# FFN up projection as seven products of halves, with the activations through DRAM and the down projection in a phase of its own

## The chip, the cores and the metric

The kernel runs on one core of a Trainium2 chip. The metric is the time of one execution in microseconds. A core has TensorE (PE in the profile; PEld are its weight loads), VectorE (DVE), ScalarE (ACT), GpSimd (POOL) and SyncE (SP), whose queue issues all DMAs here. Each engine works through its own queue in order, and semaphores make it wait for others. Products accumulate in PSUM, which has 8 banks of 512 float32 columns; all else lies in SBUF.

## The reference

It is one step of a small decoder of two layers over T = 1056 tokens (1024 of a prompt, and 8 samples of 4). Each layer has a mixer, a convolutional FFN and a gated embedding. The change is in the FFN, D = 1024 wide inside, 2 x 2816 = 5632 after the up projection:

```python
def conv_ffn(xn, prefix, w_up, conv_w, conv_b, w_down):
    L = xn.shape[1]
    u = xn @ w_up
    ext = jnp.concatenate([prefix.astype(u.dtype), u], axis=1)
    c = conv_b + ext[:, 0:L] * conv_w[0]
    for k in range(1, CONV_W):
        c = c + ext[:, k:k + L] * conv_w[k]
    gate, val = jnp.split(c, 2, axis=-1)
    return (jax.nn.gelu(gate) * val) @ w_down, ext[:, -CONV_BUF:]

xn = rmsnorm(h, W['norm_ffn'][i])
f, cstate = conv_ffn(xn, cpre, W['w_up'][i], W['conv_w'][i], W['conv_b'][i], W['w_down'][i])
h = h + f
```

## The kernel before

Everything is kept with features on the 128 partitions and tokens along the free axis. The state `h` is 8 tiles of 128 x 1056 in SBUF; its gained copy is kept as a high part `xh` and a low part `xl` (rounded to fp32r and the rest), and weights are split into `wh` and `wl` in the same way by `split` (L140 on ScalarE, L141 on VectorE). A product of two float32 matrices is then three matmuls: wh with xh, wh with xl, wl with xh. The norm's factor `R` per token is applied when a product is taken out of PSUM.

`product` (L157) makes one output tile of 128 features over three chunks of C = 352 tokens in three PSUM banks: for each of the k input tiles and each of the three terms, three matmuls of 352 columns. `product1` (L163 to L165) makes one chunk after the other, where a stage begins or ends.

`ffn` runs over 11 groups g. A group has two units; `unit(i)` makes gate tile i and value tile 22 + i:

- `up` loads 1024 x 128 of `w_up` (512 KB), splits it, makes 72 matmuls into one of two three-bank PSUM tiles `mm`, and VectorE multiplies them by R into `ext` (L563, L565, L566). GpSimd copies the conv's state columns (L568 to L570).
- `conv` starts on ScalarE (L574) and adds two taps on VectorE (L576). The gate's result goes through gelu (L582), VectorE multiplies gate by value (L585), and the activation is split into `ah` and `al` (L588, L589, L592), which stay in SBUF.

Between the two units of a group, `down(g - 1)` multiplies the activations of the group before by two rows of 128 of `w_down`: 8 output tiles of 18 matmuls, each added to h by VectorE (L624). The last `down` runs chunk by chunk with the next norm (`finish`, `factor`). `embed` and `cached_keys` turn small inputs beside the groups.

Layer 0's FFN follows the pooling mixer, whose last step (`chunk`, L366 to L381) adds to h and makes xh and xl and the squares for the norm. Layer 1's follows the attention's output projection, in which the last of 8 tiles is done chunk by chunk and `finish` is called for all 8 tiles behind it. GpSimd adds the squares (L221, L381). Within the stages a scheduler orders each engine's queue by program order and its own forecast of when inputs are ready; the list `late` holds back the first weight blocks behind the pooling.

## Time and profile before

| | us |
|---|---|
| median of 3 runs (2300.02 to 2303.77) | 2303.06 |
| the profiled execution | 2297.09 |
| its span, first to last instruction | 2295.3 |
| TensorE busy / weight loads | 2257.1 / 2209.3 |
| VectorE busy | 1368.8 |
| ScalarE busy | 820.5 |
| GpSimd busy | 458.2 |
| mean granted TensorE clock | 0.993 |

The layers' FFNs lie at about 95 to 850 us and 1385 to 2160 us. Busy shares are averages over stages with different limits, so the engines are read by stretches. A matmul's own duration includes the time that it shares with its neighbours; what one costs is the distance between the starts of two.

### The profile page before, as it was taken

The numbers are of one execution on the slowest core, as the hardware profiler recorded it, in microseconds if no ns is written. First come the engines' busy times: TensorE is split into PE (matmuls) and PEld (weight loads), VectorE is DVE, ScalarE is ACT, GpSimd is POOL, SyncE is SP. The second block draws the span as 40 slices with busy tenths as digits, with TensorE's granted clock in tenths as the row PEclk, the third lists the DMA queues.
The fourth block names the chain that finished last, engine by engine and source line by source line (L and its number), as shares of the span: only waits on it lengthen the run. The fifth ranks groups of instructions, "written<-read, shape, count | busy, mean of one in ns | idle before, by whom it ended". The sixth has DMA issues, their size and how long they took to land.

```text
span 2295.3 us, 34410 instructions
## 1 busy us (share of the span) xinstructions
PE 2257.1 (98%) x14037; PEld 2209.3 (96%) x14037; DVE 1368.8 (60%) x2122; ACT 820.5 (36%) x1489; POOL 458.2 (20%) x584
## 2 busy tenths in 40 slices
...
DMA packets 199265, 133.09 MB, mean 58 GB/s; under 512 B 36356, under 2 KB 183509, under 8 KB 198940
## 3 DMA queue, kind: packets, MB, share of 16 engines
...
## 4 chain that ended last, share of the span: by engine, by line
PE 84%; DVE 8%; ACT 3%; DMA 1%; POOL 1%; issue 1%; SPq 0%; ACTq 0%; POOLq 0%; DVEq 0%
PE mm L157 65%; DVE xl L212 2%; PE ub L163 2%; PE ub L164 2%; PE ub L165 2%; PE qkp L163 1%; PE qkp L165 1%; PE qkp L164 1%; PE dps L320 1%; DVE wl L141 1%; DVE h L634 1%; ACT e L964 1%; PE aux L163 1%; PE aux L165 1%; PE aux L164 1%
## 5 line engine op out<-in xcount | busy, mean ns | idle before, releaser
L157 PE MATMUL mm<-xh,wh 128*128 128x352 f32 x2208 | 477.4, 324 | 0.4 <-DVE ext L566 0.4
L157 PE MATMUL mm<-xh,wl 128*128 128x352 f32 x2208 | 476.3, 323 | 0.2 <-DVE wl L141 0.2
L157 PE MATMUL mm<-xl,wh 128*128 128x352 f32 x2208 | 475.5, 323 | 0.0
L140 ACT ACTIVATE wh<-wr 128x1024 fp32r<-128x1024 f32 x166 | 175.7, 1059 | 739.8 <-PE mm L157 623.4
L157 PEld LDWEIGHTS mm<-xh,wl 128*128 128x128 f32 x2208 | 378.9, 188 | 0.7 <-DVE wl L141 0.5
L157 PEld LDWEIGHTS mm<-xh,wh 128*128 128x128 f32 x2208 | 375.9, 189 | 0.7 <-issue 0.6
L157 PEld LDWEIGHTS mm<-xl,wh 128*128 128x128 f32 x2208 | 374.8, 188 | 0.6 <-issue 0.6
L563 DVE TENSOR_TENSOR ext<-mm,R 128x704 f32<-128x704 f32 x88 | 78.5, 892 | 474.9 <-PE mm L157 466.8
L569 POOL COPY sto<-ext 128x2 f32<-128x2 f32 x88 | 103.7, 1178 | 970.9 <-DVE ext L565 970.9
L624 DVE TENSOR_TENSOR h<-mm,h 128x1056 f32<-128x1056 f32 x160 | 200.9, 1256 | 115.7 <-PE mm L157 115.1
L141 DVE TENSOR_TENSOR wl<-wr,wh 128x1024 fp32r<-128x1024 f32 x164 | 204.2, 1246 | 9.6 <-ACT wh L140 8.9
L157 PE MATMUL mm<-ah,wh 128*128 128x352 f32 x960 | 208.1, 325 | 0.0
L157 PE MATMUL mm<-al,wh 128*128 128x352 f32 x960 | 207.3, 324 | 0.0
L157 PE MATMUL mm<-ah,wl 128*128 128x352 f32 x960 | 205.8, 323 | 0.0
L157 PEld LDWEIGHTS mm<-ah,wl 128*128 128x128 f32 x960 | 163.6, 188 | 0.0
L157 PEld LDWEIGHTS mm<-al,wh 128*128 128x128 f32 x960 | 163.3, 188 | 0.0
L157 PEld LDWEIGHTS mm<-ah,wh 128*128 128x128 f32 x960 | 162.3, 188 | 0.3
L163 PE MATMUL ub<-xh,wh 128*128 128x352 f32 x432 | 141.9, 328 | 0.1
L165 PE MATMUL ub<-xh,wl 128*128 128x352 f32 x432 | 140.1, 324 | 0.0
L164 PE MATMUL ub<-xl,wh 128*128 128x352 f32 x432 | 139.0, 322 | 0.0
L221 POOL TENSOR_TENSOR acc<-acc,sq 128x352 f32<-128x352 f32 x84 | 94.5, 1127 | 195.8 <-ACT sq L220 193.5
L576 DVE SCALAR_TENSOR_TENSOR cg<-ext,cw,cg 128x1072 f32<-128x1072 f32 x88 | 117.4, 1334 | 16.1 <-ACT cg L574 14.7
...
## 6 DMA issues: line engine op xcount, KB each, us to landing
...
```

The source lines that it names most:

```text
L140: A.activation(out=wh, in_=flat, func=AF.Copy)
L141: (low or V).tensor_tensor(out=wl, in0=flat, in1=wh.bitcast(F32), op=ALU.subtract)
L157: PE.matmul(ps[:, c, :C], w[k], b[k][:, c * C:(c + 1) * C], start=st, stop=sp)
L163: PE.matmul(ps, wh[k], bh[k][:, cs], start=k == 0, stop=False)
L164: PE.matmul(ps, wh[k], bl[k][:, cs], start=False, stop=False)
L165: PE.matmul(ps, wl[k], bh[k][:, cs], start=False, stop=k == nk - 1)
L212: V.scalar_tensor_tensor(out=xl[:, m, cs], in0=hm, scalar=gains[:, gain, m:m + 1], in1=xh[:, m, cs].bitcast(F32), op0=ALU.mult, op1=ALU.su ...
L221: G.tensor_tensor(out=st["acc"][:, cs], in0=st["acc"][:, cs], in1=sq, op=ALU.add)
L563: V.tensor_tensor(out=e[:, 2:2 + 2 * C].rearrange("p (c n) -> p c n", n=C), in0=ps[:, 0:2, :C], in1=R[:, :2 * C].rearrange("p (c n) -> p c ...
L569: G.tensor_copy(out=sto[:, j, 0:2], in_=e[:, NP:NP + 2])
L576: V.scalar_tensor_tensor(out=c, in0=e[:, k:k + CO], scalar=cw[:, k, j:j + 1], in1=c, op0=ALU.mult, op1=ALU.add)
L624: V.tensor_tensor(out=three(f.h[:, m, :]), in0=ps[:, :, :C], in1=three(f.h[:, m, :]), op=ALU.add)
```

## The change

The up product of a unit, gate tile over value tile, is a 2 x 2 block product: the 256 output features are two blocks, the 1024 input features two halves of four k tiles, and the tokens two halves of H = 528 (N1, N2). Seven products of halves with sums take the place of eight. GpSimd makes the four sums of weight halves, VectorE the four sums of token halves (`token_sums`, once per layer, into xh, xl, the buffers of h and `t4h`, `t4l`), and all sums are split into high and low parts. A product (`prod`) is 24 matmuls of HC = 264 columns into a PSUM tile of two banks; there are three such tiles, x, y and z, and two products accumulate in each before it is used again. ScalarE copies two products, VectorE adds and multiplies by R, and GpSimd multiplies the second token half by R (`second`).

The activation of each unit is stored in DRAM (`ad`). All 22 units of a layer run first; then the buffers of the up phase are given up, h is read back from `hd` (its SBUF held token sums meanwhile; the pooling and the output projection now store it there), and the 11 down groups run in a phase of their own, each reading its two activations back and splitting them (`act_in`). h is kept as four tiles of two features each (`hm_`) for this. In the output projection, the squares for the norm are taken tile by tile. What `up` and the old `unit` held is left out here.

```diff
+    def kept(m, c):
+        return slice(c * C, (c + 1) * C if m >= DT // 2 else min((c + 1) * C, H))
+    def high_part(f, m, cs, gain):
+        return A.activation(out=xh[:, m, cs], in_=hm_(f, m)[:, cs], func=AF.Identity, scale=gains[:, gain, m:m + 1])
+    def low_part(f, m, cs, gain):
+        V.scalar_tensor_tensor(out=xl[:, m, cs], in0=hm_(f, m)[:, cs], scalar=gains[:, gain, m:m + 1],
+                               in1=xh[:, m, cs].bitcast(F32), op0=ALU.mult, op1=ALU.subtract)
...
                 for m in ms:
-                    act = A.activation(out=xh[:, m, cs], in_=f.h[:, m, cs], func=AF.Identity, scale=gains[:, g_ffn[0], m:m + 1])
+                    dma(hd[m, :, cs], hm_(f, m)[:, cs])
+                for m in ms:
+                    if c < 2 or m >= DT // 2:
+                        act = high_part(f, m, kept(m, c), g_ffn[0])
...
+        sch, scl = wide("sch"), wide("scl")
+        t4h, t4l = [fp.tile([P, 4, H], F32R, name=n) for n in ("t4h", "t4l")]
+        vh, vl = wide("vh", 512), wide("vl", 512)
+        for n in ("p1", "p5", "u2", "vv"):
+            wide(n, H, F32)
+        exts = [fp.tile([P, EXT], F32, name=f"ext{i}") for i in range(2)]
+        wide("cg", CO, F32)
+        wide("S", 2048, F32)
+        sin = fp.tile([P, UT, 16], F32, name="sin", tag="sin", bufs=1)
+        wide("cv", CO, F32)
         sto = fp.tile([P, UT, 32], F32, name="sto", tag="sto", bufs=1)
         raw = fp.tile([P, UT, 32], F32, name="stg", tag="stg", bufs=1)
...
+        x_ps, y_ps, z_ps = [us.tile([P, 2, 512], F32, name=n)[:, :, :HC] for n in "xyz"]
...
+        def after_late():
+            es = ExitStack()
+            for ins in late:
+                es.enter_context(tc.issue_after(ins.ins))
+            return es
+        def parts_of(src, h_, l_):
+            A.activation(out=h_, in_=src, func=AF.Copy)
+            V.tensor_tensor(out=l_, in0=src, in1=h_.bitcast(F32), op=ALU.subtract)
+            return h_, l_
+        def rows(w):
+            return [x.rearrange("p (k m) -> p k m", m=P) for x in w]
+        def load(i):
+            g, v = [wp.tile([P, 1024], F32, name="wr") for _ in range(2)]
+            for x, j in ((g, i), (v, FT + i)):
+                dma(x.rearrange("p (k m) -> p k m", k=DT), a["w_up"][l].rearrange("(k p) m -> p k m", p=P)[:, :, j * P:(j + 1) * P])
+            S = wide("S", 2048, F32)
+            with after_late():
+                G.tensor_tensor(out=S[:, 0:512], in0=v[:, A1], in1=v[:, A2], op=ALU.add)
+                G.tensor_tensor(out=S[:, 512:1024], in0=S[:, 0:512], in1=g[:, A1], op=ALU.subtract)
+                G.tensor_tensor(out=S[:, 1024:1536], in0=g[:, A1], in1=v[:, A1], op=ALU.subtract)
+                G.tensor_tensor(out=S[:, 1536:2048], in0=g[:, A2], in1=S[:, 512:1024], op=ALU.subtract)
+            return g, v, S
+        def gate_parts(w):
+            with after_late():
+                return rows(parts_of(w[0], wp.tile([P, 1024], F32R, name="wh"), wp.tile([P, 1024], F32R, name="wl")))
+        def s34_parts(w):
+            with after_late():
+                return rows(parts_of(w[2][:, 1024:2048], wp.tile([P, 1024], F32R, name="wh"), wp.tile([P, 1024], F32R, name="wl")))
+        def s12_parts(w):
+            with after_late():
+                return rows(parts_of(w[2][:, 0:1024], wide("sch"), wide("scl")))
+        def val_parts(w):
+            with after_late():
+                return rows(parts_of(w[1][:, A2], wide("vh", 512), wide("vl", 512)))
+        def token_sums():
+            for k in range(4):
+                K = k + 4
+                gK = gains[:, gain, K:K + 1]
+                b = wide2("act")
+                A.activation(out=b, in_=hm_(f, k), func=AF.Identity, scale=gains[:, gain, k:k + 1])
+                ta, tb = exts if k % 2 else (wide("cg", CO, F32), wide("cv", CO, F32))
+                t1, t2, t3, t4 = ta[:, 2:2 + H], ta[:, 2 + H:2 + T], tb[:, 2:2 + H], tb[:, 2 + H:2 + T]
+                V.tensor_tensor(out=t1, in0=b[:, N2], in1=b[:, N1], op=ALU.subtract)
+                V.scalar_tensor_tensor(out=t2, in0=hm_(f, K)[:, N2], scalar=gK, in1=t1, op0=ALU.mult, op1=ALU.subtract)
+                V.scalar_tensor_tensor(out=t3, in0=hm_(f, K)[:, N2], scalar=gK, in1=b[:, N2], op0=ALU.mult, op1=ALU.subtract)
+                V.scalar_tensor_tensor(out=t4, in0=hm_(f, K)[:, N1], scalar=gK, in1=t2, op0=ALU.mult, op1=ALU.subtract)
+                tk = f.hp.tile([P, 2, T], F32R, name="tk", tag="h", bufs=4)
+                tks.append(tk)
+                for t, h_, l_, eng in ((t1, xh[:, k, N2], xl[:, k, N2], G), (t2, tk[:, 0, N1], tk[:, 0, N2], V),
+                                       (t3, tk[:, 1, N1], tk[:, 1, N2], G), (t4, t4h[:, k, :], t4l[:, k, :], V)):
+                    A.activation(out=h_, in_=t, func=AF.Copy)
+                    eng.tensor_tensor(out=l_, in0=t, in1=h_.bitcast(F32), op=ALU.subtract)
+        def wide2(name):
+            return fp.tile([P, T], F32, name=name, tag=name, bufs=2)
+        B11 = ([xh[:, k, N1] for k in range(4)], [xl[:, k, N1] for k in range(4)])
+        B21 = ([xh[:, k, N1] for k in range(4, 8)], [xl[:, k, N1] for k in range(4, 8)])
+        B22 = ([xh[:, k, N2] for k in range(4, 8)], [xl[:, k, N2] for k in range(4, 8)])
+        T1 = ([xh[:, k, N2] for k in range(4)], [xl[:, k, N2] for k in range(4)])
+        T2, T3 = [([], []), ([], [])]
+        T4 = ([t4h[:, k, :] for k in range(4)], [t4l[:, k, :] for k in range(4)])
+        def prod(ps, w, k0, b, first, by_chunk=False):
+            terms = [(k, x, y) for k in range(4) for x, y in ((w[0], b[0]), (w[0], b[1]), (w[1], b[0]))]
+            order = [(n, c) for c in range(2) for n in range(12)] if by_chunk else [(n, c) for n in range(12) for c in range(2)]
+            for n, c in order:
+                k, x, y = terms[n]
+                PE.matmul(ps[:, c, :], x[:, k0 + k, :], y[k][:, c * HC:(c + 1) * HC], start=first and n == 0, stop=n == 11,
+                          skip_group_check=True)
+        def unit(i, wa, wc, wb, wv):
+            R = f.R
+            R1, R2, RS = two(R[:, N1]), R[:, H:NP], R[:, NP:].rearrange("p (s t) -> p s t", t=LS)
+            ew, ev = exts
+            nxt_w = []
+            def tmp(n):
+                return wide(n, H, F32)
+            def second(j, e, src):
+                es = e[:, 2 + NP:].rearrange("p (s u) -> p s u", u=6)
+                G.tensor_tensor(out=e[:, 2 + H:2 + NP], in0=src[:, :NP - H], in1=R2, op=ALU.mult)
+                G.tensor_tensor(out=es[:, :, 2:6], in0=src[:, NP - H:].rearrange("p (s t) -> p s t", t=LS), in1=RS, op=ALU.mult)
+                G.tensor_copy(out=es[:, :, 0:2], in_=sin[:, j, :].rearrange("p (s r) -> p s r", r=2))
+                G.tensor_copy(out=sto[:, j, 0:2], in_=e[:, NP:NP + 2])
+                G.tensor_copy(out=sto[:, j, 2:18].rearrange("p (s r) -> p s r", r=2), in_=es[:, :, 4:6])
+            p1, p5, u2, vv = [tmp(n) for n in ("p1", "p5", "u2", "vv")]
+            more = i + 1 < FT
+            prod(x_ps, wa, 0, B11, True, i == 0)
+            A.activation(out=two(p1), in_=x_ps, func=AF.Copy)
+            if more:
+                raw_w = load(i + 1)
+            if i:
+                prod(y_ps, wc, 4, T2, True)
+                V.tensor_tensor(out=two(u2), in0=y_ps, in1=two(p1), op=ALU.add)
+                prod(z_ps, wc, 0, T1, True)
+                A.activation(out=two(p5), in_=z_ps, func=AF.Copy)
+                if more:
+                    wc_ = s12_parts(raw_w)
+                prod(x_ps, wa, 4, B21, False)
+                V.tensor_tensor(out=two(ew[:, 2:2 + H]), in0=x_ps, in1=R1, op=ALU.mult)
+                if more:
+                    wa_ = gate_parts(raw_w)
+                prod(y_ps, wb, 0, T3, False)
+            else:
+                prod(z_ps, wb, 4, B22, True)
+                A.activation(out=two(p5), in_=z_ps, func=AF.Copy)
+                prod(x_ps, wa, 4, B21, False)
+                V.tensor_tensor(out=two(ew[:, 2:2 + H]), in0=x_ps, in1=R1, op=ALU.mult)
+                wa_ = gate_parts(raw_w)
+                prod(z_ps, wc, 0, T1, False)
+                V.tensor_tensor(out=two(p5), in0=z_ps, in1=two(p5), op=ALU.subtract)
+                prod(y_ps, wc, 4, T2, True)
+                V.tensor_tensor(out=two(u2), in0=y_ps, in1=two(p1), op=ALU.add)
+                wc_ = s12_parts(raw_w)
+                prod(y_ps, wb, 0, T3, False)
+            V.tensor_tensor(out=two(vv), in0=y_ps, in1=two(p1), op=ALU.add)
+            V.tensor_tensor(out=vv, in0=vv, in1=p5, op=ALU.add)
+            second(FT + i, ev, vv)
+            if i:
+                prod(z_ps, wb, 4, B22, False)
+            V.tensor_tensor(out=two(u2), in0=z_ps, in1=two(u2), op=ALU.add)
+            second(i, ew, u2)
+            if more:
+                wb_ = s34_parts(raw_w)
+            prod(y_ps, wv, 0, T4, False)
+            V.tensor_tensor(out=two(p1), in0=y_ps, in1=two(p1), op=ALU.add)
+            V.tensor_tensor(out=ev[:, 2:2 + H], in0=p1, in1=R[:, N1], op=ALU.mult)
+            if more:
+                wv_ = val_parts(raw_w)
+            cg = conv(i, ew, "cg")
+            A.activation(out=cg, in_=cg, func=AF.Gelu_apprx_tanh)
+            cv = conv(FT + i, ev, "cv")
+            act = wide2("act")
+            V.tensor_tensor(out=act[:, :NP], in0=cg[:, :NP], in1=cv[:, :NP], op=ALU.mult)
+            V.tensor_tensor(out=act[:, NP:].rearrange("p (s t) -> p s t", t=LS), in0=bass_rows(cg), in1=bass_rows(cv), op=ALU.mult)
+            dma(ad[i], act)
+            return (wa_, wc_, wb_, wv_) if more else None
+        def conv(j, e, name):
+            c = wide(name, CO, F32)
+            A.activation(out=c, in_=e[:, 0:CO], func=AF.Identity, scale=cw[:, 0, j:j + 1], bias=cw[:, 3, j:j + 1])
+            for k in (1, 2):
+                V.scalar_tensor_tensor(out=c, in0=e[:, k:k + CO], scalar=cw[:, k, j:j + 1], in1=c, op0=ALU.mult, op1=ALU.add)
+            return c
+        def bass_rows(c):
+            v = c[:, NP + 2:CO]
+            return bass.AP(v.tensor, v.offset, [v.ap[0], [6, NS], [1, LS]])
+        w = load(0)
+        w = (gate_parts(w), s12_parts(w), s34_parts(w), val_parts(w))
+        tks = []
+        token_sums()
+        for x, q in ((T2, 0), (T3, 1)):
+            x[0].extend(t[:, q, N1] for t in tks)
+            x[1].extend(t[:, q, N2] for t in tks)
...
+        late.clear()
+        for i in range(FT):
+            w = unit(i, *w)
+        V.transpose(raw.rearrange("p t c -> p (t c)"), sto.rearrange("p t c -> p (t c)"))
+        dp = o["conv_p"][l, 0].rearrange("r (t q c) -> q r t c", q=4, c=32)
+        ds = o["conv_s"][l].rearrange("s r (t q c) -> q (s r) t c", q=4, c=32)
+        pairs(f)
+        for m in range(DT):
+            dma(hm_(f, m), hd[m])
+        for q in range(4):
+            dma(dp[q], raw[32 * q:32 * q + 2])
+            dma(ds[q], raw[32 * q + 2:32 * q + 18])
+        fes.close()
+        ues.close()
...
+        def act_in(i):
+            r = dn.tile([P, T], F32, name="ar", tag="ar", bufs=2)
+            dma(r, ad[i])
+            ah, al = [tp.tile([P, T], F32R, name=n, tag="aa", bufs=8) for n in ("ah", "al")]
+            acts[i] = parts_of(r, ah, al)
...
         ng = FT // 2
         for g in range(ng):
+            act_in(2 * g)
+            act_in(2 * g + 1)
             if g in (2, 3, 4):
-                embed(l, f, fp, range(3 * g - 6, 3 * g - 3))
+                embed(l, f, dn, range(3 * g - 6, 3 * g - 3))
             if l == 0 and g in (5, 6):
                 for j in range(2):
-                    cached_keys(f, fp, g - 5, j)
-            unit(2 * g)
-            late.clear()
-            if g and g < ng - 1:
+                    cached_keys(f, dn, g - 5, j)
+            if g:
+                if g == ng - 1:
+                    des.close()
                 down(g - 1, False)
-            unit(2 * g + 1)
-        down(ng - 2, False)
-        V.transpose(raw.rearrange("p t c -> p (t c)"), sto.rearrange("p t c -> p (t c)"))
-        dp = o["conv_p"][l, 0].rearrange("r (t q c) -> q r t c", q=4, c=32)
-        ds = o["conv_s"][l].rearrange("s r (t q c) -> q (s r) t c", q=4, c=32)
-        for q in range(4):
-            dma(dp[q], raw[32 * q:32 * q + 2])
-            dma(ds[q], raw[32 * q + 2:32 * q + 18])
-        fes.close()
         down(ng - 1, True)
+        return tp
 
 
     def embed(l, f, fp, ts):
@@ -699,7 +896,7 @@
 
     def ple_start(l, f, fp):
 
-        parts = [[fp.tile([P, T], F32R, name=n, tag=n, bufs=4) for _ in range(2)] for n in ("ah", "al")]
+        parts = [[fp.tile([P, T], F32R, name=n, tag="aa", bufs=8) for _ in range(2)] for n in ("ah", "al")]
...
                     product(ps, *ops)
-                    V.tensor_tensor(out=three(f.h[:, m, :]), in0=ps[:, :, :C], in1=three(f.h[:, m, :]), op=ALU.add)
+                    V.tensor_tensor(out=three(hm_(f, m)), in0=ps[:, :, :C], in1=three(hm_(f, m)), op=ALU.add)
+                    dma(hd[m], hm_(f, m))
+                    for c in range(3):
+                        finish(f, fp, m, c, None, st)
                     continue
...
-                        finish(f, fp, i, c, g_ffn[1], st)
+                        if c < 2 or i >= DT // 2:
+                            high_part(f, i, kept(i, c), g_ffn[1])
+                            low_part(f, i, kept(i, c), g_ffn[1])
                     factor(f, fp, st, c)
```

## Rows read from the trace of the kernel before

**Rows 1.** The page: busy by engine; the chain that ended last, by engine.
```profile
PE 2257.1 (98%) x14037; PEld 2209.3 (96%) x14037; DVE 1368.8 (60%) x2122; ACT 820.5 (36%) x1489; POOL 458.2 (20%) x584
...
PE 84%; DVE 8%; ACT 3%; DMA 1%; POOL 1%; issue 1%; SPq 0%; ACTq 0%; POOLq 0%; DVEq 0%
```
**Rows 2.** Windows, FFN of layer 0: length; busy PE, PEld, DVE, ACT, POOL; PEclk, DMA, GB/s.
```profile
300.00:400.00 100.00, 100.00 (x621) 100.00 (x620) 58.49 (x62) 23.05 (x23) 10.32 (x18) 1.00 0.16 48
```
**Rows 3.** Waits of TensorE, 150 to 850 us: in all, times, longest us.
```profile
PE ub L163 <- DVE h L624: 0.4, 1, 0.4
```
**Rows 4.** Timeline of TensorE, products of 352 columns, first and last of 73 groups: start, us.
```profile
411.00 0.65 PE L157 MATMUL mm<-xh,wh 128*128 128x352 f32 x3
...
445.96 0.65 PE L157 MATMUL mm<-xh,wh 128*128 128x352 f32 x3
```
**Rows 5.** Timeline of TensorE, products of 256 columns, first and last of 23.
```profile
1004.53 0.28 PE L816 MATMUL vps<-er,xh 128*128 128x256 f32 x1
...
1007.10 0.28 PE L817 MATMUL vps<-er,xl 128*128 128x256 f32 x1
```
**Rows 6.** Groups of instructions by line and shape: count, busy us, mean ns; idle before.
```profile
L141 DVE TENSOR_TENSOR wl<-wr,wh 128x1024 fp32r<-128x1024 f32 x164 | 204.2, 1246 | 9.6 <-ACT wh L140 8.9 <-PE ops L1014 0.7
L624 DVE TENSOR_TENSOR h<-mm,h 128x1056 f32<-128x1056 f32 x160 | 200.9, 1256 | 115.7 <-PE mm L157 115.1
L140 ACT ACTIVATE wh<-wr 128x1024 fp32r<-128x1024 f32 x166 | 175.7, 1059 | 739.8 <-PE mm L157 623.4 <-issue 67.8 <-PE ub L164 23.1
L576 DVE SCALAR_TENSOR_TENSOR cg<-ext,cw,cg 128x1072 f32<-128x1072 f32 x88 | 117.4, 1334 | 16.1 <-ACT cg L574 14.7
...
L563 DVE TENSOR_TENSOR ext<-mm,R 128x704 f32<-128x704 f32 x88 | 78.5, 892 | 474.9 <-PE mm L157 466.8 <-issue 8.1
...
L574 ACT ACTIVATE cv<-ext,cw 128x1072 f32<-128x1072 f32 x44 | 56.6, 1286 | 35.7 <-DVE ext L566 35.7
...
L589 DVE TENSOR_TENSOR al<-cv,ah 128x1024 fp32r<-128x1024 f32 x44 | 53.9, 1225 | 26.1 <-ACT ah L588 26.1
...
L565 DVE TENSOR_TENSOR ext<-mm,R 128x320 f32<-128x320 f32 x88 | 42.3, 481 | 0.0
...
L570 POOL COPY sto<-ext 128x16 f32<-128x16 f32 x88 | 17.1, 194 | 0.0
...
L592 DVE TENSOR_TENSOR al<-cv,ah 128x32 fp32r<-128x32 f32 x44 | 8.2, 186 | 0.0
```
**Rows 7.** Timeline of VectorE, then GpSimd, in the attention: start, us [idle before].
```profile
1201.99 0.69 DVE L992 TENSOR_TENSOR wl<-trp,wh 128x512 fp32r<-128x512 f32 x1
1202.60 0.95 DVE L954 SCALAR_TENSOR_TENSOR sm<-sm,nsink 128x4 f32<-128x4 f32 x1
...
1204.35 0.13 DVE L958 TENSOR_TENSOR sm<-sm,nsink 128x4 f32<-128x4 f32 x1
...
1202.24 1.29 POOL L1024 TENSOR_TENSOR xl<-rbs,xh 128x512 fp32r<-128x512 f32 x1 [1.52 <-ACT xh L1023]
```
**Rows 8.** Timeline of TensorE, GpSimd and VectorE where layer 0's FFN begins.
```profile
95.29 0.32 PE L163 MATMUL mm<-xh,wh 128*128 128x352 f32 x1
...
96.08 6.04 POOL L381 TENSOR_TENSOR acc<-acc,sq 128x352 f32<-128x352 f32 x5 [0.85 <-ACT sq L379]
...
96.96 3.16 DVE L375 SCALAR_TENSOR_TENSOR xl<-h,gains,xh 128x352 fp32r<-128x352 f32 x3
...
100.47 2.02 DVE L375 SCALAR_TENSOR_TENSOR xl<-h,gains,xh 128x352 fp32r<-128x352 f32 x2
...
120.40 0.89 DVE L563 TENSOR_TENSOR ext<-mm,R 128x704 f32<-128x704 f32 x1 [8.12 <-issue]
```
**Rows 9.** Windows, while h is read from DRAM: last column GB/s.
```profile
1304.00:1308.00 4.00, 4.00 (x27) 4.00 (x26) 0.83 (x1) 1.06 (x1) 0.00 (x0) 1.00 1.00 402
```
**Rows 10.** Windows, the end of the output projection, columns as in rows 2.
```profile
1380.00:1385.00 5.00, 5.00 (x34) 5.00 (x33) 5.00 (x11) 5.00 (x12) 1.45 (x1) 1.00 0.37 108
```
**Rows 11.** Windows, the end of the pooling and the attention, columns as in rows 2.
```profile
80.00:85.00 5.00, 5.00 (x23) 4.60 (x21) 3.81 (x7) 2.20 (x5) 1.87 (x2) 0.61 0.00 0
...
1200.00:1300.00 100.00, 91.01 (x607) 75.35 (x606) 89.73 (x340) 90.48 (x293) 66.65 (x99) 1.00 0.14 43
```

135 lines of the change are left out of this document (56 added, 79 removed).

## Prediction

> **What bounds the kernel now.** I read the busy shares first, then the chain that ended last, then the two FFN stages by stretches of 100 us, then who waits for whom. TensorE is busy for 98% of the span and carries 84% of the chain [rows 1]. In the FFN stretches it is 100% busy at the full granted clock, while VectorE stands at 58%, ScalarE at 23% and GpSimd at 10% [rows 2]; from 150 to 850 us the longest wait that TensorE had is 0.4 us, once [rows 3]. So in this stage only TensorE's own work sets the time: a product that goes is time that goes, and any other engine may grow until it becomes the bound instead. The profiled execution took 2297.1 us (span 2295.3); the median of the runs is 2303.1, 0.26% above it. I sum against 2297.1.
>
> **The products.** Before, an up tile is 8 k x 3 terms x 3 chunks = 72 matmuls of 352 columns; 88 tiles make 6336. Between 411.00 and 445.96 there are 216 of them, 161.8 ns apart [rows 4]: 6336 x 161.8 = 1025.2 us. After, a pair of tiles (a unit) is 7 products x 4 k x 3 terms x 2 chunks = 168 matmuls of 264 columns, 7392 in all. There are 7/8 of the columns, but 17% more instructions, each with its weight load, so the question is what 264 columns cost. No row has 264. The nearest are the 256-column products, which also load a weight each: 22 steps from 1004.53 to 1007.10 make 116.8 ns [rows 5]. Bounds are therefore 116.8 and 161.8; less is excluded by the row of fewer columns. A straight line between them is 0.469 ns a column, and 264 stands next to 256: 120.5 ns. 7392 x 120.5 = 890.8 us, **134.4 us less** (the lower bound would give 162 less). A unit is then 168 x 0.1205 = 20.24 us of TensorE. The Trainium skill (TensorE: Matmul & The Clock Gate, Back-to-back issue gap) gives 81 ns between matmuls of 128 columns in a stream of weight loads and matmuls and 131 ns at 512; an estimate on its straight line is 98.7 ns at 264 and 110.2 at 352, and the term would be 31 us more instead of 134 less. The trace does not agree: 352 columns already take 161.8 here.
>
> **The other engines in a unit** (durations from [rows 6]). Before, a pair of tiles gave VectorE 19.9 us in TensorE's 216 x 0.1618 = 34.9, of which four down evacuations of 1.256. After, without those: five evacuations of 528 columns from PSUM, 0.71 each between the rows of 320 (0.481) and 704 (0.892): 3.5; two operations of 528 on SBUF, 1.4; three low parts of 1024 at 1.246 and one of 512 at 0.69 [rows 7]: 4.4; four conv taps at 1.333: 5.3; the product of gate and value, 1.225 + 0.186: 1.4. That is 16.1, and 15.1 once the overlap of neighbours is taken off (the operation at 1202.60 starts 0.61 after one of 0.69 [rows 7]; 13 such pairs at 0.08). ScalarE: two copies of 528 and one of 512 at some 0.6 and three of 1024 at 1.06, two conv starts and a gelu at up to 1.29: 8.8. Both fit under 20.24.
>
> GpSimd is new: four sums of 512 at 1.29 [rows 7], two products of 496 at 1.25, two of 32 at an estimated 0.3, six small copies at 0.194: 9.4 us. It would fit alone, but it does not run alone. A VectorE operation of 4 elements with both inputs in SBUF took 0.95 us (0.13 for one like it with GpSimd idle) and ended 0.02 after the GpSimd difference that was running; L992, which reads PSUM and lay over its start, kept its 0.69 [rows 7]. And where the two queues met, five GpSimd additions took 6.04 us, 1.2 each, and VectorE's five beside them 3.16 + 2.02, 1.0 each, for 352 columns, where 320 take 0.481 [rows 6, 8]. So the two exclude each other, except while VectorE reads PSUM. One addition of 352 holds the other engine for about 0.81 (1.2 of period less 0.38 for VectorE's own 352 at the 1.07 ns a column between the rows of 320 and 704); scaled, a unit's GpSimd work holds 7.9 us. VectorE has 15.1 + 7.9 = 23.0 if nothing overlaps, and 3.2 of this (the PSUM reads) may. Bounds for the **tax on TensorE per unit**: 0 (20.24 us has 5.1 us of VectorE idle and 3.2 of PSUM reads for GpSimd's 7.9) and 23.0 - 20.2 = 2.8. I take half of the PSUM reads as overlapped: 21.4, a tax of 1.1 us, for 42 units (the first of each layer is counted below): **+46**. It would show as TensorE waiting for VectorE, with three PSUM tiles that are each needed again one to three products (2.9 us each) later.
>
> **Weights and DMA.** A unit loads 2 x 512 KB and stores 528 KB per 21 us, 74 GB/s; the chip moved 400 GB/s when eight 528 KB loads were issued together [rows 9]. The store of an activation stands on SP's queue before or behind the next weight load and waits for the conv chain; a load issued 8 us into a unit still leaves its parts 12 us. Cost 0; without that cover, one load of some 3 us per unit.
>
> **Entry to each FFN.** The first unit needs sums of tokens: per k one ScalarE scaling, four VectorE sums of 528, two low parts on VectorE, two on GpSimd: 4 x 6 x 0.7 = 16.6 us of VectorE and 8 x 1.2 = 9.6 of GpSimd against each other, 26 in all. Before, TensorE begins the up products at 95.29, while VectorE still makes low parts until 102.5 [rows 8], and the first two tiles are done at 120.4. After, three products (8.7 us) don't need the sums and run from the same moment; the sums end at about 97 + 3 + 26 = 126 and the last products trail them. Against 95.3 + 8.7 that is 22 us, with nearly two products done meanwhile: 15 us lost. In layer 1 VectorE is full from 1380 on as well [rows 10], but sums of six of the eight rows can start earlier: 10. Bounds per layer 0 and 26. **+25**.
>
> **Exit.** Behind the last unit the conv chain (1.3 + 2.7 + 1.1 + 2.7 + 1.4) runs with no product over it, but the first down group needs activations 0 and 1, stored 20 units before, and buffers of which the first is free three products earlier; one low part (1.25) and a reload of h (8 x 528 KB at up to 402 GB/s [rows 9], 11 us or more, begun before the end and needed one row per 2.9 us) stand in the way. I take 5 per layer, between 0 and the whole chain and a load, some 13: **+10**. The down phase has 144 matmuls x 161.8 = 23.3 us a group as before, over 15.1 of VectorE (eight evacuations of 1.256, four low parts) and 90 GB/s: no cost, no gain. The finer copies of the pooling, the squares moved ahead in the output projection and the stores of h lie beside TensorE: +2.
>
> **Sum:** 2297.1 - 134.4 + 46 + 25 + 10 + 2 = 2245.7; against the runs' median up to 6 more. I say 2248.
>
> **Rivals.** *A, the port decides:* GpSimd and VectorE exclude each other almost wholly and the up phase runs at their sum, 23.0 us a unit or more. Without a tax the sum is 2199.7, so it turns at 97.4 / 42 = 2.3 us of tax, a unit of 22.6. At 23.0 the time is 2316, at 24 it is 2358: slower. For it speaks the sum of the two queues, 13% over TensorE's; against it the attention, where VectorE was 90% and GpSimd 67% busy and TensorE still 91% [rows 11]. The Trainium skill (SBUF — State Buffer, Who interferes with whom) states this as a rule: an exclusive lock between a GpSimd instruction that reads SBUF and a VectorE one with two SBUF inputs, held for the whole instruction. The trace agrees, by the 0.95 us above. *B, the port is hidden:* GpSimd falls into VectorE's idle time and TensorE stays the bound; 2200. *C, the boundaries cost what they can:* 26 at each entry, 13 at each exit, and a lower clock behind them (it stood at 0.61 in a stretch behind sparse products [rows 11]), 5 us: 2297.1 - 134.4 + 46 + 78 + 5 + 2 = 2294: no change. *D, the products don't shrink:* at 139 ns or more for 264 columns the gain is gone, about 2380; the 256-column row is strongly against it.
>
> **Chances.** My forecast 0.52, A 0.24, B 0.16, C 0.06, D 0.02. 0.2% (5 us) is about what a measurement of this kernel can tell from no change. Faster takes the forecast, B and a little of C: 0.70; slower A, D and part of C: 0.25; same 0.05. The range leaves out less than half of A and D above and a little of B below: 2198 to 2325. The forecast alone reaches from 2215 to 2280 (tax 0.4 to 1.9).
>
> **What would show it.** Right: 264-column matmuls 120 ns apart; units of 21 to 22 us; TensorE waiting for VectorE's evacuations; VectorE over 85% busy with low parts and taps stretched by up to 1.2 us; 10 to 15 us of thin TensorE at each entry. Wrong: TensorE at 100% in the up phase (B), units above 22.6 (A), or long idle stretches where the phases meet (C).

## The result, and the profile after

The changed kernel takes 2357.1 us (median of 4 runs, 2351.3 to 2359.6) against 2302.5 before on the same chip: 1.0235 times as long, 95% interval 1.0213 to 1.0256. It is **slower**, above the predicted range, and 109 us above the predicted 2248. The page's busy times and its chain by engine, which answer to [rows 1]:

```profile
PE 2187.7 (93%) x15093; PEld 2121.9 (90%) x15093; DVE 1673.4 (71%) x2307; ACT 951.5 (40%) x1662; POOL 840.0 (36%) x950
...
PE 42%; DVE 21%; POOL 16%; issue 8%; ACT 8%; DMA 4%; SPq 0%; ACTq 0%; POOLq 0%; DVEq 0%
```

TensorE is busy 69 us less, but holds half of the chain that it held. Windows of the changed kernel (columns as in [rows 2]): the units, the two entries from the first product to the first T4 product, the two exits:

```profile
300.00:400.00 100.00, 94.27 (x764) 93.22 (x764) 80.59 (x80) 37.27 (x41) 54.47 (x63) 1.00 0.23 76
107.20:160.90 53.70, 34.56 (x200) 31.14 (x199) 48.77 (x52) 25.50 (x40) 37.15 (x32) 0.75 0.49 108
1422.30:1478.20 55.90, 33.91 (x196) 31.25 (x195) 50.55 (x55) 25.23 (x37) 34.12 (x28) 0.76 0.27 45
620.00:640.00 20.00, 1.30 (x8) 1.09 (x8) 10.90 (x11) 4.76 (x5) 1.48 (x4) 0.65 0.91 291
1940.00:1958.00 18.00, 0.21 (x1) 0.21 (x2) 9.57 (x10) 4.46 (x5) 0.00 (x0) 0.60 0.92 288
```

In the units no engine is full, which points to a chain that runs in a ring rather than to a bound of throughput. At the boundaries TensorE stands, and its granted clock is low around it (0.75, 0.76, 0.65 and 0.60 in these rows). Its waits from 150 to 850 us (in all, times, longest), against 0.4 us in [rows 3]:

```profile
PE y L670 <- DVE vv L723: 21.3, 18, 1.4
PE mm L162 <- ACT ah L599: 18.7, 1, 18.7
```

And the products themselves, which answer to [rows 4, 5] (start, us; 46 matmuls lie between the two starts):

```profile
411.21 0.40 PE L670 MATMUL x<-xh,wh 128*128 128x264 f32 x2
...
416.85 0.40 PE L670 MATMUL z<-xh,wl 128*128 128x264 f32 x2
```

5.64 / 46 = 122.6 ns; I take 122 for the units.

**The balance**, in the two profiled spans (2295.3 and 2356.6). The starts of layer 0's products run from 107.2 to 620.6 us, of layer 1's from 1422.3 to 1939.1; down starts at 639.6 and 1957.8. An exit's gap is counted from the start of the last product to the start of down.

| term | predicted | measured | how |
|---|---|---|---|
| products | -134 | -123 | 7392 x 122 ns less 6336 x 161.8 ns |
| tax in the units | +46 | +66 | behind the first T4, 459.7 and 460.9 us for 3504 matmuls, which are 427.5 |
| entries | +25 | +63 | 53.7 and 55.9 us for 192 matmuls, which are 23.4 |
| exits | +10 | +38 | 19.0 and 18.7 us |
| pooling, other stages | +2 | +12 | first product at 107.2 instead of 95.3 |
| low clock behind the exits | 0 | +6 | down's products run at 0.50 for 3.4 us in layer 0 and for 6.2 and 3.4 in layer 1; half of 13.0 |
| sum | -51 | +62 | spans: +61.3 |

Down's products at the low clock (columns as in [rows 2]); in the kernel before the granted clock is 1.00 from 1390 to 2290 us:

```profile
639.60:643.00 3.40, 3.40 (x13) 3.33 (x14) 3.12 (x4) 2.58 (x5) 0.00 (x0) 0.50 0.57 146
1957.80:1964.00 6.20, 6.20 (x22) 6.13 (x23) 3.46 (x5) 3.66 (x6) 0.00 (x0) 0.50 0.60 147
1970.80:1974.20 3.40, 3.40 (x14) 3.40 (x13) 0.27 (x1) 0.00 (x0) 0.00 (x0) 0.50 0.81 266
```

**The ring.** One unit of the changed kernel lasts 22.0 us. VectorE, GpSimd, SyncE and the end of TensorE's T3 product in one of them (timelines: start, us [idle before]):

```profile
406.57 0.69 DVE L600 TENSOR_TENSOR vl<-wr,vh 128x512 fp32r<-128x512 f32 x1
...
411.65 1.92 DVE L741 TENSOR_TENSOR act<-cg,cv 128x1024 f32<-128x1024 f32 x1
413.50 1.28 DVE L742 TENSOR_TENSOR act<-cg,cv 128x32 f32<-128x32 f32 x1
...
417.24 1.32 DVE L600 TENSOR_TENSOR scl<-S,sch 128x1024 fp32r<-128x1024 f32 x1 [1.84 <-ACT sch L599]
418.49 1.21 DVE L600 TENSOR_TENSOR wl<-wr,wh 128x1024 fp32r<-128x1024 f32 x1
419.63 0.70 DVE L723 TENSOR_TENSOR vv<-y,p 128x528 f32<-128x528 f32 x1
...
428.51 0.68 DVE L600 TENSOR_TENSOR vl<-wr,vh 128x512 fp32r<-128x512 f32 x1
```

```profile
411.20 1.29 POOL L613 TENSOR_TENSOR S<-wr 128x512 f32<-128x512 f32 x1 [1.39 <-DMA wr<-in_w_up_dram]
412.45 2.28 POOL L615 TENSOR_TENSOR S<-wr 128x512 f32<-128x512 f32 x1
414.68 0.20 POOL L688 COPY ext<-sin 128x16 f32<-128x16 f32 x1
414.83 1.29 POOL L614 TENSOR_TENSOR S<-S,wr 128x512 f32<-128x512 f32 x1
```

```profile
407.28 0.37 SPq L101 DMA_DIRECT2D wr<-in_w_up_dram  x1
```

```profile
415.39 0.40 PE L670 MATMUL y<-tk,wl 128*128 128x264 f32 x2
```

The value low part (406.57) is the last reader of a raw buffer; 0.02 us behind it SyncE issues the next load; it lands at 411.2; GpSimd makes the sums that sch needs until 416.1, having lost 1 us to VectorE (2.28 instead of 1.29); ScalarE makes sch; VectorE makes scl and wl, and **behind these two in its queue** stands vv, whose product ended at 415.8. VectorE was idle for 1.84 us ahead of scl, for the last 1.4 of them with vv ready. T4 goes into the same PSUM tile and waits 1.4 us for vv; its evacuation and the taps stand ahead of the next value low part, at 428.51. The Trainium skill (TensorE: Matmul & The Clock Gate, Architectural detail: the array is 16× 32×32, not 1× 128×128) says that ScalarE and VectorE take their queues strictly in order; this trace agrees, vv being ready 3.8 us before it runs (419.63).

### The profile page after: what moved, and what is told of

Read it like the earlier page. It is cut to its first block, busy times and chain, and to the rows that moved or that the text cites. A ratio compares the mean times of both kernels' runs of the same rounds, so it can differ in the third digit from the quotient of the medians.

```text
span 2356.6 us, 37870 instructions
## 1 busy us (share of the span) xinstructions
PE 2187.7 (93%) x15093; PEld 2121.9 (90%) x15093; DVE 1673.4 (71%) x2307; ACT 951.5 (40%) x1662; POOL 840.0 (36%) x950
## 4 chain that ended last, share of the span: by engine, by line
PE 42%; DVE 21%; POOL 16%; issue 8%; ACT 8%; DMA 4%; SPq 0%; ACTq 0%; POOLq 0%; DVEq 0%
PE mm L162 22%; POOL ext L686 4%; POOL S L615 3%; DVE wl L600 2%; POOL ext L687 2%; DVE xl L229 2%; POOL S L614 2%; DMA wr<-in_w_up_dram 2%; PE ub L168 2%; PE ub L170 2%; PE ub L169 2%; ACT cg L748 2%; DVE cg L750 2%; ACT sch L599 2%; POOL S L613 2%
## 5 line engine op out<-in xcount | busy, mean ns | idle before, releaser
L145 ACT ACTIVATE wh<-wr 128x1024 fp32r<-128x1024 f32 x78 | 82.2, 1055 | 265.3 <-PE mm L162 213.9
L670 PE MATMUL x<-xh,wh 128*128 128x264 f32 x704 | 149.5, 293 | 15.9 <-ACT p L695 14.8
L670 PE MATMUL x<-xh,wl 128*128 128x264 f32 x704 | 148.7, 291 | 3.2 <-DVE wl L600 3.2
L748 ACT ACTIVATE cg<-ext,cw 128x1072 f32<-128x1072 f32 x44 | 56.5, 1284 | 234.6 <-POOL ext L687 234.6
L670 PE MATMUL x<-xl,wh 128*128 128x264 f32 x704 | 147.7, 290 | 0.0
L599 ACT ACTIVATE sch<-S 128x1024 fp32r<-128x1024 f32 x44 | 46.7, 1061 | 227.7 <-POOL S L614 218.3
L670 PEld LDWEIGHTS x<-xh,wh 128*128 128x128 f32 x704 | 112.6, 194 | 19.8 <-ACT p L695 17.3
L670 PE MATMUL y<-tk,sch 128*128 128x264 f32 x704 | 118.5, 289 | 12.7 <-DVE tk L653 8.9
L688 POOL COPY ext<-sin 128x16 f32<-128x16 f32 x88 | 56.1, 638 | 193.2 <-DVE cg L750 180.8
L599 ACT ACTIVATE ah<-ar 128x1056 fp32r<-128x1056 f32 x44 | 47.8, 1087 | 184.9 <-PE mm L162 155.6
```

Source lines behind the costliest of these rows:

```text
L145: A.activation(out=wh, in_=flat, func=AF.Copy)
L599: A.activation(out=h_, in_=src, func=AF.Copy)
L670: PE.matmul(ps[:, c, :], x[:, k0 + k, :], y[k][:, c * HC:(c + 1) * HC], start=first and n == 0, stop=n == 11, skip_group_check=True)
L748: A.activation(out=c, in_=e[:, 0:CO], func=AF.Identity, scale=cw[:, 0, j:j + 1], bias=cw[:, 3, j:j + 1])
```

## The experiments

The theories at the start: a *ring* through queues and buffers in the units (against the *port*, GpSimd and VectorE having no room), and *order and buffers* at the boundaries (against sheer work, or the clock). All in one table: ratios to the kernel before; the unit's period and the gap at the exit are given for layers 0 / 1, the entry is first product to first T4. Periods are those of the units behind the first few of a layer.

| kernel | median us | ratio to before, 95% interval | unit us | entry us | gap us |
|---|---|---|---|---|---|
| changed | 2357.1 | 1.0213 to 1.0256 | 22.0 / 22.0 | 54 / 56 | 19.0 / 18.7 |
| s1_value_buffer | 2327.4 | 1.0089 to 1.0131 | 21.3 / 21.3 | 58 / 55 | 18.0 / 18.8 |
| s2_vv_first | 2352.5 | 1.0195 to 1.0236 | 22.0 / 21.9 | 55 / 57 | 18.9 / 18.7 |
| s1u_queue_order | 2316.8 | 1.0045 to 1.0075 | 20.3 to 21.3 / 20.55 | 58 / 55 | 18.4 / 20.8 |
| s2f_vv_forced | 2302.2 | 0.9989 to 1.0008 | 20.5 / 20.5 | 55 / 55 | 18.2 / 17.9 |
| s1lock_one_more | 2382.7 | 1.0317 to 1.0368 | 22.4 / 22.4 | 59 / 57 | 19.9 / 18.7 |
| c1lock_one_more | 2330.6 | 1.0109 to 1.0140 | 21.1 to 21.8 / 21.4 to 21.8 | 55 / 57 | 6.6 / 6.5 |
| s2flock_one_more | 2307.7 | 1.0011 to 1.0034 | 20.5 / 20.5 | 54 / 55 | 19.2 / 19.3 |
| e1_exit | 2341.8 | 1.0147 to 1.0183 | 22.0 / 21.9 | 56 / 58 | 14.2 / 13.5 |
| e1b_exit_forced | 2334.1 | 1.0119 to 1.0149 | 21.9 / 21.9 | 55 / 57 | 8.4 / 8.4 |
| c1_ring_and_exit | 2286.4 | 0.9909 to 0.9941 | 20.3 to 21.3 / 20.5 | 55 / 57 | 6.4 / 3.2 |
| c2_early_sums | 2290.1 | 0.9916 to 0.9955 | 20.2 to 21.3 / 20.5 | 56 / 57 | 6.5 / 5.3 |
| b1_order_and_exit | 2279.9 | 0.9890 to 0.9928 | 20.5 / 20.5 | 55 / 58 | 6.5 / 6.6 |
| e2_entry_layout | 2357.0 | 1.0218 to 1.0252 | 22.0 / 22.0 | 56 / 57 | 18.9 / 19.4 |
| v_lows_entry | 2358.9 | 1.0230 to 1.0266 | 21.9 / 22.0 | 57 / 56 | 18.9 / 18.6 |
| nolow_entry | 2340.7 | 1.0154 to 1.0185 | 21.8 / 21.8 | 45 / 47 | 18.8 / 18.7 |
| h1_late_stores | 2351.8 | 1.0204 to 1.0238 | 21.9 / 22.0 | 55 / 56 | 19.3 / 18.5 |

### The units

**s1_value_buffer.**

```diff
-            g, v = [wp.tile([P, 1024], F32, name="wr") for _ in range(2)]
+            g, v = wp.tile([P, 1024], F32, name="wr"), fp.tile([P, 1024], F32, name="vr", tag="vr", bufs=2)
```

> Edit: the raw value weights get a double buffer of their own, so that the load of unit i+1 no longer waits until the low part of unit i's value weights has been read. Loop theory (a ring through SyncE, the load, GpSimd's four sums, ScalarE, VectorE's in-order queue and TensorE's T4 product sets the 22.0 us of a unit): the ring opens, the period falls from 22.0 to 20.5-20.9 us, the time from 2357 by 42 x 1.1-1.5 = 46-63 to 2294-2311. Port theory (GpSimd and VectorE excluding each other leave no room for a shorter unit): the work of both engines is the same, the period stays at 21.8-22.1 us and the time at 2348-2360. Clock theory: as the port theory.

30 us, and a period that is 21.30 in every unit from the sixth on: about half of what the ring theory asked. A second ring took over, TensorE's T3 product now waiting for the evacuation u, 0.6 us in a unit. VectorE's timeline of it:

```profile
427.32 2.69 DVE L752 SCALAR_TENSOR_TENSOR cv<-ext,cw,cv 128x1072 f32<-128x1072 f32 x2
429.93 0.70 DVE L702 TENSOR_TENSOR u<-y,p 128x528 f32<-128x528 f32 x1
```

**s2_vv_first** moves two lines in the program, the parts of the next weights behind vv.

> Edit: order alone. The high and low parts of the next S1, S2 and gate weights are issued behind the evacuation of the T3 product instead of ahead of it, so that the evacuation is not queued behind them on VectorE. Loop theory: the 1.2-1.4 us per unit that T4's start waits for vv goes, the period falls to 20.6-21.2 us, the time by 35-60 to 2297-2322. Port theory: the same instructions hold the same port as long, period 21.8-22.1 us, time 2348-2360. If another part of the ring takes over (the value low part still gates the load), about half: 21.3-21.6 us.

VectorE's order stayed as it was, since the scheduler sorts by its own forecast, and vv is still behind scl and wl in the trace. The run tells nothing on the ring; it was made again below.

**s1u_queue_order** takes the second ring away.

```diff
+                with tc.issue_after(made.ins):
+                    tail(i - 1)
```

> Edit on top of s1_value_buffer (period 21.30 us, constant over units): the value half's taps, product and store of the unit before are queued on VectorE behind the evacuation of the T2 product instead of ahead of it. Queue theory (with the load's ring open, TensorE's T3 product waits 0.6 us per unit for that evacuation, which stands behind 2.7 us of taps in VectorE's queue): the wait goes, the period falls to 20.6-20.9 us (168 products x 122 ns = 20.5), the time from 2327 by 42 x 0.4-0.7 = 17-29 to 2298-2310. Port theory (VectorE, 86% busy with its stretched instructions, is the bound): 21.2-21.4 us and 2322-2330.

Here `made` is the evacuation u, and `tail` the value half's taps, product and store. 10.6 us, less than asked: layer 1 runs at 20.55, TensorE without a break, but layer 0 ran at 20.2 to 20.4 for eleven units and then at 21.3 for eight, with the same instructions. In the slower eight TensorE waits for vv again (3.8 us in seven waits from 430 to 590 us). c1 and c2, which have these units, change pace at the same place. What moves vv there is open.

**s1lock_one_more** asks for the port's price.

```diff
+            G.tensor_tensor(out=p5[:, 0:512], in0=u2[:, 0:512], in1=p5[:, 0:512], op=ALU.add)
```

> Edit on top of s1_value_buffer: one more GpSimd addition of two 512-column operands per unit (its result is read by nothing), behind the gate half's second product with the factor; GpSimd is 61% busy there. Port theory: each such addition keeps VectorE out for up to its 1.28 us, so the period grows from 21.30 by 0.8-1.3 to 22.1-22.6 us and the time by 34-55 to 2361-2382. Queue theory (only what stands in the ring counts; the addition stands beside it): at most 0.3 us, 2327-2340.

1.07 us a unit, as the port theory said: TensorE's wait for u grew from 0.6 to 1.6 us. The time grew by 55 us, 45 of them in the units, to just above that theory's range. GpSimd and VectorE beside the added line (L732):

```profile
416.27 1.29 POOL L732 TENSOR_TENSOR p<-u,p 128x512 f32<-128x512 f32 x1
...
418.91 2.32 POOL L617 TENSOR_TENSOR S<-wr,vr 128x512 f32<-128x512 f32 x1
```

```profile
420.00 1.80 DVE L737 TENSOR_TENSOR ext<-p,R 128x528 f32<-128x528 f32 x1
...
424.61 3.73 DVE L753 SCALAR_TENSOR_TENSOR cv<-ext,cw,cv 128x1072 f32<-128x1072 f32 x2
428.26 0.70 DVE L702 TENSOR_TENSOR u<-y,p 128x528 f32<-128x528 f32 x1
```

GpSimd's sums come a step later and so meet other VectorE instructions: the evacuation's second half takes 1.80 instead of 0.70, the taps 3.73 instead of 2.69, and both stand ahead of u, for which TensorE waits. So the exclusion is real, but this does not yet say whether it is a bound or a longer link.

**s2f_vv_forced** repeats s2 with the order held:

```diff
+            if i and more:
+                with tc.issue_after(made.ins):
+                    wc_ = s12_parts(raw_w)
+                    wa_ = gate_parts(raw_w)
```

> Edit on the changed kernel, with its single set of buffers for the raw weights: the high and low parts of the next S1, S2 and gate weights are queued on VectorE behind the two operations that make vv (s2_vv_first left that order as it was). Ring theory (22.0 us are the way around load, GpSimd's sums, ScalarE, VectorE's queue, TensorE's T4 product; an evacuation that no longer stands behind two low parts shortens it by their 2.4 us): the period falls to 20.5-21.3 us and the time from 2357 by 30-60 to 2297-2327. Port theory (VectorE's and GpSimd's work sets 22.0): 21.8-22.1 us, 2349-2360.

Here `made` is vv's second operation. With nothing but two low parts behind vv instead of ahead of it on VectorE, **nearly all of the tax is gone**: 55 us, 20.5 us a unit in both layers, and by the balance's count 7 us of tax where 66 were. VectorE's timeline of it, and the window of the units:

```profile
399.59 0.71 DVE L719 TENSOR_TENSOR vv<-y,p 128x528 f32<-128x528 f32 x1 [0.40 <-PE y L670]
...
401.02 1.22 DVE L600 TENSOR_TENSOR scl<-S,sch 128x1024 fp32r<-128x1024 f32 x1
402.16 2.28 DVE L600 TENSOR_TENSOR wl<-wr,wh 128x1024 fp32r<-128x1024 f32 x1
```

```profile
300.00:400.00 100.00, 100.00 (x821) 100.00 (x821) 93.07 (x83) 41.62 (x45) 77.57 (x70) 1.00 0.24 78
```

VectorE and GpSimd are fuller than in the changed kernel (93% and 78% against 81% and 54%, since more units lie in 100 us and more instructions meet), and TensorE waits for neither. vv now starts as soon as its product has ended.

**c1lock_one_more and s2flock_one_more** put the same additional line into two kernels whose TensorE was full.

> Edit on top of c1_ring_and_exit, where TensorE is 100% busy in the units: the same additional GpSimd addition of 512 columns per unit as in s1lock_one_more (read by nothing). Port as a bound of throughput: VectorE (85% busy) and GpSimd (73%) have no room left, the period grows from 20.5-21.3 by 0.8-1.3 us as it did there, the time from 2286 by 34-55 to 2320-2341. Port as a stretch of single links only: the units stay within 0.4 us of c1's, 2286-2303.

> Edit on top of s2f_vv_forced: the same additional GpSimd addition of 512 columns per unit. Sum theory (what GpSimd holds and what VectorE works must fit one after the other into a unit; with VectorE 93% busy there are 1.4 us left): most of the 1.07 us fits, the period grows from 20.5 to 20.6-21.1 us and the time from 2302 by 4-25 to 2306-2327. If a chain sets the unit in which the addition stands (as in s1lock_one_more and c1lock_one_more): 21.4-21.8 us, 2340-2357. If there is a new slack: under 20.6, 2300-2306.

In c1 it costs 44 us, 1.05 a unit in the mean (0.7 in layer 0, where c1 itself had slow units, and 1.2 in layer 1); there TensorE waits about as often for vv (nine times, 7.9 us, from 200 to 600 us) as for ScalarE's copy of P1 (nine times, 6.2). In s2f the units stay at 20.5 us, with GpSimd now at 89%. The time grows by 5.5 us, to just above the range of the slack theory, whose period came; in the two profiled executions layer 0's first two units are 4.3 us longer. The window of the units:

```profile
200.00:550.00 350.00, 349.95 (x2863) 349.74 (x2864) 327.67 (x291) 142.83 (x154) 310.83 (x256) 1.00 0.24 78
```

One line has three prices. As these three kernels read, the exclusion lengthens instructions, and it costs time only where a lengthened one stands between a product and the next use of its PSUM tile. As a bound of throughput it does not show up to there.

### The exits

SyncE's timeline at layer 0's exit in the changed kernel, then in e1, then in e1b (start, us):

```profile
623.18 8.44 SPq L101 DMA_DIRECT2D out_dram<-stg  x8
631.73 0.56 SPq L101 DMA_DIRECT2D ad<-act  x1
632.38 2.14 SPq L101 DMA_DIRECT2D ar<-ad  x2
```

```profile
623.61 5.36 SPq L101 DMA_DIRECT2D out_dram<-stg  x4
629.01 1.53 SPq L101 DMA_DIRECT2D ar<-ad  x2
```

```profile
618.06 0.93 SPq L101 DMA_DIRECT2D ar<-ad  x2
619.10 5.97 SPq L101 DMA_DIRECT2D h<-hd  x8
```

**e1_exit** traces the first two inputs of down ahead of the last unit's `tail` and the stores, and lays early tiles under them; **e1b_exit_forced** holds that order on SyncE.

```diff
+        act_in(0)
+        got = act_in(1)
+        with tc.issue_after(got.ins):
+            for m in range(DT):
+                dma(hm_(f, m), hd[m])
+        act = tail(FT - 1, dn.tile([P, T], F32, name="ar", tag="ar", bufs=2))
```

> Edit: at the end of the up phase the first two loads and splits of activations stand ahead of the last unit's convolution, its store, and the eight stores of the convolution state, and the tiles they reuse are ones that are read for the last time early. Queue theory (the 18.9 us without a product at the exit of each layer are SyncE's in-order queue, the stores ahead of the loads, and the buffers they reuse): the gap falls to 3-6 us, the time by 26-32 to 2325-2331. Rival (the last unit's convolution and gelu on VectorE and ScalarE are the bound): the gap stays over 10 us and the time falls by at most 16, to 2341 or more. Units' period unchanged at 22.0 us.

> Edit on top of e1_exit (gap 14.2 and 13.5 us): the scheduler had put four of the state's stores and the eight loads of h ahead of the two loads of activations on SyncE; here they are queued behind them. Queue theory: the loads are issued at about 616 instead of 629 us and land in 3 us, the gap falls to 4-7 us in both layers, the time from 2342 by 14-20 to 2322-2328. Rival (VectorE's work at the end of the last unit, 9.5 of 10 us busy in 620 to 630, is the bound): the gap stays over 10 us, 2335-2342.

Products ended at 621; the loads that down begins with were issued at 632.4, behind eight stores of the convolution state and the last activation's store, which waits for the last convolution. The scheduler had left four stores ahead in e1 (14 us); with the order held the gap is 8.4, and ScalarE's gelu of the last unit stands ahead of the split. So the order of this queue was 10 of the 19 us.

**c1_ring_and_exit and b1_order_and_exit** combine: s1u's units, or s2f's, with the exit and the last tail queued behind the first splits.

> Edits together: the double buffer of the value weights and the queue order of s1u_queue_order, the exit of e1b_exit_forced, and the last unit's convolution queued behind the first two splits of activations; the tiles that those splits write lie where the last unit reads early. If the two costs are separate (ring and port in the units, queue order at the exits): units at 20.5 us (TensorE's products), gaps of 3-5 us in both layers; from s1u_queue_order's 2317 fall 18.4 + 20.8 - 8 = 31 us, to 2282-2290, 0.5-0.9% under the kernel before. If the exit's gap has another floor (VectorE's last evacuations): gaps of 8 us, 2290-2298. The entries stay at 53-58 us from the first product to the first T4.

> Edits together: the forced order of s2f_vv_forced (units of 20.5 us, TensorE 100% busy) and the exit of e1b_exit_forced with the last unit's convolution queued behind the first two splits. If the two costs are separate: units stay at 20.5 us, the gaps fall from 18.2 and 17.9 us to 5-9, the time from 2302 by 18-26 to 2276-2284, 0.8-1.1% under the kernel before. If VectorE, 93% busy with nothing queued idle, has no room for the moved tail: gaps over 10 us, 2286 or more.

The two costs are separate and add. b1 takes 2279.9 us, **0.9909 of the kernel before** (0.9890 to 0.9928), with the same arithmetic as the changed kernel; c1 takes 2286.4. **c2_early_sums** lets layer 0's first sums and parts go ahead of the pooling on top of c1; the first T4 was to come 5 to 10 us earlier if they bound the entry. The entry stayed (55.9 us against 55.2), and so did the time (2290.1).

With the last tail behind the split, b1's gap is 6.5 us, so that tail was worth about 2 of e1b's 8.4. What is left is SyncE's queue again. SyncE's timeline in layer 0 of b1 with the first split, then SyncE's in layer 1 of c1:

```profile
583.02 7.24 SPq L101 DMA_DIRECT2D wr<-in_w_down_dram  x2
590.32 0.94 SPq L101 DMA_DIRECT2D ar<-ad  x2
594.72 1.08 ACT L605 ACTIVATE ah<-ar 128x1056 fp32r<-128x1056 f32 x1 [7.11 <-DMA ar<-ad]
```

```profile
1882.28 0.37 SPq L101 DMA_DIRECT2D wr<-in_w_down_dram  x1
1882.70 0.97 SPq L101 DMA_DIRECT2D ar<-ad  x2
```

The second of the two loads of `w_down` waits for the low part on VectorE that frees its buffer and ends at 589.87, and the loads of activations stand behind it: they are issued 1 us after the last product began (589.36), and the first split starts 4.4 us later. In layer 1 of c1 that low part ended at 1882.25, the loads were issued 2.9 us ahead of the last product (1885.59), and the gap is 3.2 us. No run put these loads ahead of those of `w_down`; this is read from the two traces.

### The entries

**e2_entry_layout** allocates `act` lower, **v_lows_entry** makes all low parts of the token sums on VectorE, **nolow_entry** leaves them out:

> Edit: one block of tiles is moved in the layout of the up phase, so that the scaled activations of the token sums no longer lie where the row factor before them still works. Aliasing theory (the token sums start 12 us late, since their first tile overlaps the factor's scratch): the first token sum starts at 107-110 us instead of 119.7, the first T4 product at 148-152 instead of 160.9, layer 1 likewise, the time falls by 16-24 to 2333-2341. Rival (the sums are bound by ScalarE, VectorE and GpSimd, and by the slow clock that the entry makes): less than 5 us per layer, 2347-2357.

> Edit on the changed kernel: in the token sums the 8 low parts per layer that GpSimd makes are made by VectorE. Port theory of the entry (VectorE is busy without a break from 1436 to 1471 us, 34.9 us for instructions that cost 23 us where GpSimd is idle): the 5.4 us of work that VectorE gets are less than what GpSimd's 8 additions of 1.2-1.9 us stretch its instructions by, the first T4 product comes 2-6 us earlier per layer, 2345-2353. Rival (VectorE's count of instructions is the bound of the entry): 4-6 us later per layer, 2365-2369.

> Edit on the changed kernel: the 16 low parts of the token sums per layer are left out, 8 on VectorE and 8 on GpSimd; the products take the high parts in their place, so their number and length stay. VectorE theory of the entry (VectorE is busy for the whole 54 us from the first product to the first T4 in each layer: 39 us of its own work and 14 us of stretch by GpSimd's two-operand additions): VectorE loses 8 x 0.67 = 5.4 us of work and up to 8 x 1.07 = 8.6 us of stretch, the first T4 comes 8-14 us earlier after the first product, in both layers, and the time falls by 16-28 to 2329-2341. Rival (TensorE's low clock and the order of ScalarE's queue set the entry): less than 5 us per layer, 2347-2357.

The layout freed the scaled activations (10.1 us behind the first product instead of 12.5), and the entry did not shorten: aliasing was not the bound. In ScalarE's queue of that kernel these activations (L643) stand behind the norm's factor (L180), ahead of which ScalarE was idle:

```profile
109.86 0.56 ACT L180 ACTIVATE rt<-aux,eps 128x352 f32<-128x352 f32 x1 [5.15 <-DVE R L185]
...
111.88 2.23 ACT L643 ACTIVATE act<-h,gains 128x1056 f32<-128x1056 f32 x2
```

Whether the sums could go ahead of the factor was not tried; this queue is a rival that stays open. Moving 8 low parts from GpSimd to VectorE was worth nothing either way: VectorE was busy for 47.9 us there, against 48.8. Leaving all 16 out shortens the entry by 9 us in both layers. The windows of nolow's two entries:

```profile
103.80:148.70 44.90, 30.80 (x199) 27.69 (x198) 34.54 (x43) 23.83 (x39) 21.34 (x19) 0.81 0.56 129
1414.80:1462.20 47.40, 29.53 (x196) 27.61 (x195) 37.63 (x47) 24.85 (x37) 20.45 (x20) 0.82 0.31 53
```

VectorE falls from 48.8 to 34.5 us, the entry only from 53.7 to 44.9, so VectorE (91% busy before, 77% here) stops being the one bound, and what else holds the entry is not shown. The expectation called it busy throughout; that was the sum of durations, and by the window it is 91%. Of the 30 us that the changed kernel's entry loses, 19 are TensorE idle and 11 are busy time beyond the 23.4 us of its products at full speed (34.6 us, of which 2.8 are other small matmuls), at a mean granted clock of 0.75. The clock fell to its lower level, 0.50, while TensorE stood between the first products.

**h1_late_stores** takes the 24 stores of h out of the pooling.

> Edit on the changed kernel: in layer 0 the 24 stores of h by thirds of a row inside the pooling are left out of it and 8 stores of whole rows stand behind the pooling, ahead of the token sums. Store theory of the longer pooling (its end came at 107 instead of 95 us): the first product starts at 95-100 us and the time falls by 5-10. Rival (the granted clock, 0.50 for 20 to 52 us in the changed kernel's profile and for 20 to 28 us before, which has nothing to do with the stores): the first product starts at 101-107 us as in the other runs with the same pooling, and the token sums wait for the stores, so that the time is 2352-2365.

The first product starts at 101.3 us, as in others with the old stores. What it does go with is the granted clock up to there. Windows of the kernel before, of the changed one, and of h1, from the start to the first product:

```profile
0.00:95.30 95.30, 89.19 (x498) 79.76 (x499) 68.65 (x138) 64.65 (x141) 30.31 (x31) 0.86 0.32 101
```

```profile
0.00:107.20 107.20, 101.41 (x497) 89.59 (x498) 65.94 (x147) 63.25 (x146) 24.60 (x30) 0.76 0.36 116
```

```profile
0.00:101.30 101.30, 94.74 (x497) 83.23 (x498) 64.33 (x147) 62.97 (x146) 24.63 (x30) 0.81 0.34 109
```

95.3 x 0.86 = 82.0, 107.2 x 0.76 = 81.5 and 101.3 x 0.81 = 82.1 us: counted at the full clock the three stretches are equally long, so the 11.9 us by which the first product is late are the clock. From 15 to 55 us alone it was 0.87 before, 0.57 in the changed kernel and 0.79 in h1; kernels with one and the same pooling show 0.57 to 0.79 there.

## Why the prediction failed, step by step

The sum missed by 113 us: 38 in the entries, 28 in the exits, 20 in the tax, 11 in the products, 10 in the pooling and 6 in the low clock behind the exits.

- **The products** were right in kind: 122 ns instead of 120.5, -123 instead of -134. Rival D is out. On the page's line between 128 and 512 columns in the Trainium skill (TensorE: Matmul & The Clock Gate, Back-to-back issue gap) a 264-column matmul would take 98.7 ns, an estimate; the trace does not agree.
- **The tax** was near in size (+46 for +66) and wrong in kind. The step "the two exclude each other ... 21.4, a tax of 1.1 us" made a sum of two queues out of it. s2f has the same work and 7 us of tax; s2flock has more work and the same period. What cost 1.5 us a unit was the order of VectorE's queue, with the load's ring behind it. The step "a load issued 8 us into a unit still leaves its parts 12 us. Cost 0" failed: the load is issued where the value low part ends, and its parts come just where vv is due. Rival B, the hidden port, was true of the instructions, and not of the order in which they were queued. Rival A's sign came, but its mechanism, the bound of both engines, did not: the units stayed under its 22.6 us. Of the signs named for the forecast, VectorE over 85% busy did not come (81%).
- **The entries** were the largest miss, +63 for +25. The step "4 x 6 x 0.7 = 16.6 of VectorE ... 26 in all" priced the token sums alone. They took 24.1 us of VectorE in layer 0, stretched by GpSimd's instructions, so that price was near; but they began 13.7 us behind the first product, where "about 97 + 3" had them 4.7 behind it, and were spread over 31.8 us. VectorE's queue there also holds the parts of the first unit's weights and some of the second's, the norm's factor, five evacuations and a transpose. TensorE's low clock, for which the step had no term, adds a third. Which wait ends last there stays open.
- **The exits**, +38 for +10, above the bound of 13 per layer. "Behind the last unit the conv chain ... one low part and a reload of h stand in the way" left out the eight stores on SyncE's queue and the store that waits for the chain, both ahead of the loads, and the load of `w_down` ahead of these that waits for its buffer.
- **The pooling** was to cost 2 and cost 12, by the windows above all of it in the granted clock; no step spoke of it. The only sentence on the clock, in rival C, read its 0.61 at 80 to 85 us as one "behind sparse products"; from 55 to 66.9 us, where it fell, TensorE had been busy for 11.4 of 11.9 us. Rival C saw the boundaries at 78 us together and 5 for a lower clock behind them; they measured 101 and 6, and with 20 us more of tax and 12 of pooling the time was slower, not level.
